# Elementwise binary cross entropy on one core: loads of predictions issued from SyncE instead of GpSimd

## The chip, the cores and the metric

The kernel runs on one core of one Trainium2 chip. The metric is the device time of one execution in microseconds (us); of several runs the median is given. The engines that matter here are VectorE (DVE), ScalarE (ACT), GpSimd (POOL) and SyncE (SP), and the 16 DMA engines of the core that carry all transfers between the memory (HBM) and the core's on-chip memory (SBUF, 128 partitions). An engine issues a transfer, and the transfer then stands in that engine's DMA queue.

## The reference

```
pred, target: float32 [8192, 8192]; pred in (0.01, 0.99), target 0 or 1
pred = clip(pred, 1e-7, 1 - 1e-7)
out  = -(target * log(pred) + (1 - target) * log(1 - pred))
```

With a target of 0 or 1 this is -log|target - 1 + pred|, and this form is what the kernel computes. Two inputs are read and one output is written, 268.4 MB each.

## The kernel before, in words

The 8192 x 8192 elements are taken as one flat list and cut into 39 chunks. A chunk of width w is 128 x w elements, row p of it on partition p, and contiguous in memory. Chunk 0 has w = 8192 (`first`), chunks 1 to 35 have w = 14336 (`WIDE`, called full chunks), and the last three, 36 to 38, have the widths of `TAIL`: 6656, 6656 and 1024. `z` is 35, the last full chunk.

Predictions live in `ring_p`, float32, with three slots of 14336 columns. Chunk k stands in slot k mod 3, and the three tail chunks lie side by side in one slot, that of chunk 33. All work on a chunk is done in place, and the store reads the same slot, so a slot is free again when the store of its chunk has landed. Targets live in `ring_t`, bfloat16 (the transfer converts from float32), with one single slot.

Per chunk, in two halves: `clip` (VectorE, L85), `merge` (VectorE, L91: target - 1 + pred), absolute value and logarithm (ScalarE, L94 and L95), `negate` (VectorE, L99). Then the chunk is stored (`store`, L79).

The order is written out by hand under a manual schedule: each engine carries out its instructions in the order of the text, and waits are put in where data or a slot demands them. In the loop over k the text reads: merge of chunk k, load of targets k+1 (`load_t`, L73, free to go when both merges have read the single slot), negate of k, clip of k+1, store of k, load of predictions k+2 (`load_p`, L70). Before the loop stand the loads p_0 (from ScalarE), t_0 and p_1 (from GpSimd). After it come the loads of the three tail chunks, predictions and targets in turn, the store of chunk 35, and the tail chunks' own work; their three stores (the last one in three pieces of 108, 12 and 8 rows) are issued from SyncE.

All other transfers are issued from GpSimd. Its order in the loop is thus t_k+1, s_k, p_k+2, t_k+2, s_k+1, p_k+3 and so on (t targets, s store, p predictions), one line in which each issue also waits for those ahead of it. The load p_k+2 needs the slot of chunk k-1, so it needs s_k-1 to have landed.

Of the kernel before, what the change touches and what calls it, by code (L numbers as in the profile page):

```python
# [1 line left out]

# [4 lines left out]

EPS = 1e-7

WIDE = 14336  # L10
SLOTS = 3
TAIL = (6656, 6656, 1024)
ROWS = (108, 12, 8)


@with_exitstack
def kernel(
    ctx: ExitStack,
    tc: tile.TileContext,
    pred: bass.AP,  # L20
    target: bass.AP,
    out: bass.AP,
):
    nc = tc.nc
    fp32 = mybir.dt.float32
    low = mybir.dt.bfloat16
    Alu = mybir.AluOpType
    Act = mybir.ActivationFunctionType
    P = nc.NUM_PARTITIONS

    R, C = pred.shape
    total = R * C // P
    rest = total - sum(TAIL)
    n = rest // WIDE
    first = rest - n * WIDE
    assert 0 < first <= WIDE and n > 4 and sum(TAIL) <= WIDE
    spots = [(first, 0)]
    spots += [(WIDE, k % SLOTS * WIDE) for k in range(1, n + 1)]
    c = (n + 1) % SLOTS * WIDE
    for w in TAIL:  # L40
        spots.append((w, c))
        c += w
    n = len(spots)
    z = n - 1 - len(TAIL)
    starts = [sum(w for w, _ in spots[:k]) * P for k in range(n)]

    pool = ctx.enter_context(tc.tile_pool(name="rings", bufs=1))
    ring_p = pool.tile([P, SLOTS * WIDE], fp32, name="ring_p", tag="ring_p")
    ring_t = pool.tile([P, WIDE], low, name="ring_t", tag="ring_t")
    warm = pool.tile([1, 8], fp32, name="warm", tag="warm")  # L50

    def chunk(ap, k):
        flat = ap.rearrange("r c -> (r c)")
        w = spots[k][0]
        return flat[starts[k] : starts[k] + w * P].rearrange("(p w) -> p w", p=P)

    def cols(ring, k, part, c):
        w = spots[k][0]
        i, m = part
        return ring[:, c + i * w // m : c + (i + 1) * w // m]  # L60

    def p_of(k, part=(0, 1)):
        return cols(ring_p, k, part, spots[k][1])

    def t_of(k, part=(0, 1)):
        return cols(ring_t, k, part, spots[k][1] % WIDE)

    def load_p(k):
        queue = nc.scalar if k == 0 else nc.gpsimd
        queue.dma_start(out=p_of(k), in_=chunk(pred, k))  # L70

    def load_t(k):
        nc.gpsimd.dma_start(out=t_of(k), in_=chunk(target, k))  # L73

    def store(k):
        queue = nc.sync if k > z else nc.gpsimd
        r = 0
        for rows in ROWS if k == n - 1 else (P,):
            queue.dma_start(out=chunk(out, k)[r : r + rows, :], in_=p_of(k)[r : r + rows, :])  # L79
            r += rows  # L80
        assert r == P

    def clip(k, *part):
        p = p_of(k, *part)
        nc.vector.tensor_scalar(  # L85
            out=p, in0=p, scalar1=EPS, scalar2=1 - EPS, op0=Alu.max, op1=Alu.min
        )

    def merge(k, *part):
        p, t = p_of(k, *part), t_of(k, *part)  # L90
        nc.vector.scalar_tensor_tensor(  # L91
            out=p, in0=t, scalar=1.0, in1=p, op0=Alu.subtract, op1=Alu.add
        )
        nc.scalar.activation(out=p, in_=p, func=Act.Abs)  # L94
        nc.scalar.activation(out=p, in_=p, func=Act.Ln)  # L95

    def negate(k, *part):
        p = p_of(k, *part)
        nc.vector.tensor_scalar(out=p, in0=p, scalar1=-1.0, scalar2=None, op0=Alu.mult)  # L99

    halves = (0, 2), (1, 2)
    with tc.manual_schedule():
        load_p(0)
        load_t(0)
        load_p(1)
        nc.vector.memset(warm, 1.0)  # L106
        nc.scalar.activation(out=warm, in_=warm, func=Act.Ln)  # L107
        for h in halves:
            clip(0, h)
        for k in range(z):  # L110
            for h in halves:
                merge(k, h)
            load_t(k + 1)
            for h in halves:
                negate(k, h)
            for h in halves:
                clip(k + 1, h)
            store(k)
            if k + 2 <= z:
                load_p(k + 2)  # L120
        for h in halves:
            merge(z, h)
        a, b, c = range(z + 1, n)
        for j in a, b, c:
            load_p(j)
            load_t(j)
        negate(z, halves[0])
        clip(a)
        negate(z, halves[1])
        store(z)  # L130
        merge(a)
        clip(b)
        merge(b)
        negate(a)
        store(a)
        clip(c)
        merge(c)
        negate(b)
        store(b)
        negate(c)  # L140
        store(c)


# [1 line left out]
_INS = ['pred', 'target']  # L145
_OUTS = [((8192, 8192), 'float32')]


# [23 lines left out]
```

## Time and profile before

| | before |
|---|---|
| median of 3 runs | 1867.39 us (1866.88 to 1868.22) |
| the profiled execution | 1868.84 us |
| its span (first to last instruction) | 1867.1 us |
| VectorE busy | 1118.2 us (60%) |
| ScalarE busy | 901.7 us (48%) |
| GpSimd busy | 283.3 us (15%) |
| moved by DMA | 671.14 MB, counted by what is written for the converted targets |
| issues of predictions at L70 from GpSimd | 38, median 3.82 us |
| issues of targets at L73 from GpSimd | 39, median 0.53 us |
| issues of stores at L79 from GpSimd / SyncE | 36, median 3.63 us / 5 |

How to read it: the profile is of one execution, whose own time is 1868.84 us; the span leaves out 1.7 us around the instructions. Issuing a transfer counts as busy time of GpSimd, the transfer itself does not. In a timeline a row gives the start and length in us, the engine, the line of the kernel, the operation with its tiles, and in brackets how long the engine had been idle before it and what ended that. "To landing" is the time from the issue of a transfer until its completion was signalled, so it includes the time that it stood in line. Besides these views, the trace holds a record of every DMA packet: its queue, its start, its length and its bytes. Here a packet is one row of a transfer.

### The profile page before, as it was taken

What the parts mean: (1) busy time and instruction counts of PE and PEld (TensorE: products, weight loads), DVE (VectorE), ACT (ScalarE), POOL (GpSimd) and SP (SyncE); (2) the same over time, 40 slices, a digit from 0 to 9 for tenths busy, and PEclk for the clock granted to TensorE, in tenths of its full rate; (3) what the DMA queues carried; (4) which work ended last, traced back from release to release, by engine and by line L of the source; (5) the groups of instructions that cost most, each with busy time, mean ns of one, the idle gap of its engine ahead of it and who ended that gap; (6) DMA issues with size and microseconds to landing.
All of it is one profiled execution on the core that took longest, in us unless ns stands there. A gap on an engine that the chain in (4) does not pass through costs nothing.

```text
span 1867.1 us, 695 instructions
## 1 busy us (share of the span) xinstructions
DVE 1118.2 (60%) x226; ACT 901.7 (48%) x152; POOL 283.3 (15%) x117
## 2 busy tenths in 40 slices
DVE  4675665655556555665665556655566665556664
ACT  3555444444555555444444555555544444455555
POOL 0121111111111101111111111101111111111100
DMA  9999999999999999999999999999999999999998
GB/s 331 336 373 373 364 355 359 356 355 355 354 354 359 373 373 373 370 356 362 356 354 358 354 354 356 367 373 373 373 362 360 359 354 359 354 354 354 360 366 346
DMA packets 16869, 671.14 MB, mean 359 GB/s; under 512 B 1888, under 2 KB 1888, under 8 KB 2272
## 3 DMA queue, kind: packets, MB, share of 16 engines
q0 software_dynamic: 16272, 659.56, 98.5%
q1 hardware_dynamic: 448, 7.34, 0.9%
q10 hardware_dynamic: 144, 4.19, 0.6%
q14 instruction: 5, 0.04, 0.0%
HBM read 536.87 MB, written 268.44 MB: 431 GB/s over the span
## 4 chain that ended last, share of the span: by engine, by line
DMA 67%; issue 28%; DVE 2%; ACT 2%; POOL 0%; POOLq 0%; DVEq 0%; PEldq 0%
DMA ring_t<-in_target_dram 67%; DVE ring_p L91 2%; ACT ring_p L95 1%; ACT ring_p L94 1%; DVE ring_p L99 0%; POOL out_dram L79 0%; POOL ring_p L70 0%; DVEq L167 0%; POOLq L73 0%; POOLq L79 0%; DVEq L91 0%; PEldq L167 0%
## 5 line engine op out<-in xcount | busy, mean ns | idle before, releaser
L94 ACT ACTIVATE ring_p<-ring_p 128x7168 f32<-128x7168 f32 (+3 forms) x75 | 451.6, 6021 | 943.5 <-DVE ring_p L91 943.5
L91 DVE SCALAR_TENSOR_TENSOR ring_p<-ring_t,ring_p 128x7168 f32<-128x7168 bf16 (+3 forms) x75 | 554.8, 7436 | 236.9 <-DMA ring_t<-in_target_dram 236.8
L99 DVE TENSOR_SCALAR ring_p<-ring_p 128x7168 f32<-128x7168 f32 (+3 forms) x75 | 285.0, 3801 | 475.0 <-ACT ring_p L95 475.0
L95 ACT ACTIVATE ring_p<-ring_p 128x7168 f32<-128x7168 f32 (+3 forms) x75 | 452.1, 6028 | 2.4
L85 DVE TENSOR_SCALAR ring_p<-ring_p 128x7168 f32<-128x7168 f32 (+3 forms) x75 | 281.8, 3798 | 20.1 <-DMA ring_p<-in_pred_dram 20.1
L79 POOL DMA_DIRECT2D out_dram<-ring_p x36 | 127.4, 3540 | 730.3 <-DVE ring_p L99 730.3
L73 POOL DMA_DIRECT2D ring_t<-in_target_dram x39 | 20.7, 532 | 802.9 <-DVE ring_p L91 802.1
L70 POOL DMA_DIRECT2D ring_p<-in_pred_dram x38 | 135.3, 3560 | 0.0
L107 ACT ACT_TABLE_LOAD x1 | 1.3, 1283 | 1.1 <-PEq L156 1.1
L106 DVE MEMSET warm<- 1x8 f32 x1 | 0.1, 65 | 0.8 <-PEq L156 0.8
L107 ACT ACTIVATE warm<-warm 1x8 f32<-1x8 f32 x1 | 0.2, 208 | 0.0
L156 POOL MEMSET const-float32-0.0<- 128x1 f32 x1 | 0.1, 98 | 0.2 <-issue 0.2
L156 POOL MEMSET const-bfloat16-1.0<- 128x1 bf16 x1 | 0.1, 101 | 0.0
L156 POOL MEMSET const-float32-1.0<- 128x1 f32 x1 | 0.1, 98 | 0.0
L156 POOL MEMSET const-uint8-127<- 128x1 uint8 x1 | 0.1, 98 | 0.0
## 6 DMA issues: line engine op xcount, KB each, us to landing
ring_p<-in_pred_dram POOLq DMA_DIRECT2D x35, 7168.0 KB, 44.3
out_dram<-ring_p POOLq DMA_DIRECT2D x35, 7168.0 KB, 31.0
ring_t<-in_target_dram POOLq DMA_DIRECT2D x35, 3584.0 KB, 35.2
ring_p<-in_pred_dram POOLq DMA_DIRECT2D x2, 3328.0 KB, 33.6
out_dram<-ring_p SPq DMA_DIRECT2D x2, 3328.0 KB, 15.1
ring_p<-in_pred_dram ACTq DMA_DIRECT2D x1, 4096.0 KB, 19.5
out_dram<-ring_p POOLq DMA_DIRECT2D x1, 4096.0 KB, 21.4
ring_t<-in_target_dram POOLq DMA_DIRECT2D x2, 1664.0 KB, 28.8
```

What stands on the lines that cost most here:

```text
L70: queue.dma_start(out=p_of(k), in_=chunk(pred, k))
L73: nc.gpsimd.dma_start(out=t_of(k), in_=chunk(target, k))
L79: queue.dma_start(out=chunk(out, k)[r : r + rows, :], in_=p_of(k)[r : r + rows, :])
L85: nc.vector.tensor_scalar(out=p, in0=p, scalar1=EPS, scalar2=1 - EPS, op0=Alu.max, op1=Alu.min)
L91: nc.vector.scalar_tensor_tensor(out=p, in0=t, scalar=1.0, in1=p, op0=Alu.subtract, op1=Alu.add)
L94: nc.scalar.activation(out=p, in_=p, func=Act.Abs)
L95: nc.scalar.activation(out=p, in_=p, func=Act.Ln)
L99: nc.vector.tensor_scalar(out=p, in0=p, scalar1=-1.0, scalar2=None, op0=Alu.mult)
L106: nc.vector.memset(warm, 1.0)
L107: nc.scalar.activation(out=warm, in_=warm, func=Act.Ln)
L156: nc = _bacc.Bacc("TRN2", target_bir_lowering=False, num_devices=1)
```

## The change

The predictions of chunks 2 to 35 are issued from SyncE; p_0 stays on ScalarE, p_1 and those of the three tail chunks stay on GpSimd. Targets and stores are issued as before.

```diff
     def load_p(k):
-        queue = nc.scalar if k == 0 else nc.gpsimd
+        queue = nc.scalar if k == 0 else nc.gpsimd if k == 1 or k > z else nc.sync
         queue.dma_start(out=p_of(k), in_=chunk(pred, k))
```

The orders of VectorE and ScalarE are the same in both kernels. GpSimd's list loses 34 issues and keeps the rest in order. SyncE's list begins with the 34 loads p_2 to p_35, and its stores of the tail chunks come after them. On SyncE the first of the loads, p_2, waits for nothing; each later one, p_k, waits for s_k-3, the store that frees its slot, and no longer stands behind s_k-2 as it did on GpSimd.

## The prediction

> **What bounds the kernel now.** I write p_k, t_k and s_k for the load of predictions, the load of targets and the store of chunk k. First I read the slices, the DMA queues and the HBM line of the page.
>
> ```profile
> span 1867.1 us, 695 instructions
> ...
> DMA  9999999999999999999999999999999999999998
> ...
> q0 software_dynamic: 16272, 659.56, 98.5%
> ...
> HBM read 536.87 MB, written 268.44 MB: 431 GB/s over the span
> ```
>
> The 16 DMA engines are busy in every slice, and nearly all of it is one queue, GpSimd's. VectorE (60%) and ScalarE (48%) have time to spare. Second, the timeline of a period in the steady part, from one target landing to the next:
>
> ```profile
> 306.61 15.16 DVE L91 SCALAR_TENSOR_TENSOR ring_p<-ring_t,ring_p 128x7168 f32<-128x7168 bf16 x2 [7.56 <-DMA ring_t<-in_target_dram]
> ...
> 322.06 0.53 POOL L73 DMA_DIRECT2D ring_t<-in_target_dram  x1 [22.90 <-DVE ring_p L91]
> ...
> 342.76 7.70 DVE L85 TENSOR_SCALAR ring_p<-ring_p 128x7168 f32<-128x7168 f32 x2
> 343.14 3.63 POOL L79 DMA_DIRECT2D out_dram<-ring_p  x1 [20.55 <-DVE ring_p L99]
> 346.76 3.82 POOL L70 DMA_DIRECT2D ring_p<-in_pred_dram  x1
> 357.39 15.16 DVE L91 SCALAR_TENSOR_TENSOR ring_p<-ring_t,ring_p 128x7168 f32<-128x7168 bf16 x2 [6.93 <-DMA ring_t<-in_target_dram]
> ```
>
> The reader is to see a period of 357.39 - 306.61 = 50.78 us, and three offsets from the target's landing that the change leaves alone: the next target is issued 15.45 us after it, the store 36.5 us after it, the old load of predictions 40.15 us after it. VectorE waits for the target (7 us a period), so the chain of waits is 67% "DMA ring_t". Is that target late by its own delay, or because the engines are full? The packet records decide: every DMA of 128 rows puts 8 rows on each engine; a row of 57,344 bytes takes 2.116 us, a target row (57,344 bytes read, 28,672 written) 2.130. One period is 8 x (2.116 + 2.116 + 2.130) = 50.90 us per engine, the period itself (packets overlap a little). So the steady part has no free DMA time, and nothing that is only issued earlier can shorten it. Third, the issues with time to landing:
>
> ```profile
> ring_p<-in_pred_dram POOLq DMA_DIRECT2D x35, 7168.0 KB, 44.3
> out_dram<-ring_p POOLq DMA_DIRECT2D x35, 7168.0 KB, 31.0
> ring_t<-in_target_dram POOLq DMA_DIRECT2D x35, 3584.0 KB, 35.2
> ...
> ring_p<-in_pred_dram ACTq DMA_DIRECT2D x1, 4096.0 KB, 19.5
> ...
> ring_t<-in_target_dram POOLq DMA_DIRECT2D x1, 2048.0 KB, 21.4
> ```
>
> A transfer needs 8 x 2.12 = 17 us alone; 31 to 44 us to landing means that it stands in line behind one or two others. In one line each transfer has 14 to 27 us of such cover. The last two rows are p_0 (ScalarE's queue) and t_0 (GpSimd's): 8 packets of 1.21 us each would be 9.7 us, and both took twice that, because two queues share each engine: in the packet records they alternate, one packet of each. That is the model for what follows. A packet is also chosen about one packet ahead: s_36, issued from SP at 1838.73, still saw some engines begin another packet of GpSimd's line at 1841.35, 2.6 us later, and come to it only after that.
>
> **The change, part by part.** *Removed*: 34 of the 38 issues at L70 leave GpSimd, 34 x 3.82 = 130 us of its time. Worth 0: GpSimd waits 802 us for VectorE at L73 and 730 at L79, and the engines have over 14 us of queued work whenever a store is issued. The store's 3.63 us against the target's 0.53 is time held back by the clip (342.76 to 350.46). [...]
>
> *Moved*: p_k+2 now waits on SP only for its slot, that is for s_k-1 to land. Behind it on SP stand only later predictions and the last stores. p_2 waits for nothing and starts at 0.7 us.
>
> *Start.* p_0, t_0 and p_2 now share the engines: 9.7 + 9.8 + 17 = 36.5 us from 1.8 on, so t_0 lands near 39 us (now 22.6). p_1 and t_1 follow in GpSimd's line, to 56 and 73. s_0 is issued 23.5 us after t_0's landing, at 62.5, in time, and runs from 73 to 82.7. Now both lines are empty: p_3 waits for s_0, and t_2 is issued only at 73.3 + 15.45 = 88.8. Gap 1 is landing to SP's issue (0.3 + 0.15), issue to first packet as for p_0 (0.73 to 1.74 and 2.49, so 1.0 to 1.8), and about 0.7 to 1.0 of a first packet (p_0's took 1.9 instead of 1.21): 2.5 us. p_3 and t_2 end near 119.5; s_1, issued at 110, fills 119.5 to 136.4; t_3 is issued at 119.8 + 15.45 = 135.3. How long a GpSimd issue takes to its first packet is bounded by two rows: t_0, issued at 1.23, has its first packet at 6.05 (4.8 us, in the cold start, and it had to wait its turn behind p_0); s_1, issued at 94.14, follows t_2's last packet without a gap at 100.1, 5.97 us after its issue, of which 3.62 were held back by the clip, so at most 2.4 us. I take 2, from the second, which is a warm queue. Gap 2: 135.3 + 2 - 136.4 = 0.9, with the first packet 1.5 us (0 to 4).
> [...]
>
> *Steady part.* p_4 becomes visible about 2 us after s_1 has ended, t_3 before that. So from then on the target leads by two packets (4.2 us), alternates with the predictions, and lands when these have two packets left; they fill the next store's stretch to 16.9 + 4.2 = 21.1 us after the target's last packet; the next target is visible 0.3 + 15.45 + 2 = 17.8 us after it, 3.3 us in time. This state feeds itself, and costs no gap. What it costs is the alternation: p_0's packets took 1.213 us alone and 1.226 between t_0's; 0.013 x 8 x 33 = 3.4 us. Bounds 0 and 3.4; I take 3.4.
>
> *End.* The last p from SP is p_35. With t_34 landing at 0, s_33 and the rest of p_35 run to 20.8, and t_35 alone to 37.9 (SP's line is empty). s_34 is issued only at 36.5, held back to 40.1 by the clip, first packet at about 42; p_36 stands behind it on GpSimd. Gap 3: 4 us (3, up to 6 if predictions have one packet left instead of two). Before, s_34 was issued 14 us before t_35's landing. From s_34's first packet to the end it is the same line in both kernels, full to the last stores, so the gap is not given back.
>
> **Sum** against the profiled execution (1868.84 us; span 1867.1): gaps 2.5 + 1.5 + 4 = 8.0; the gap of 1.0 us at 56 us (between t_1 and s_0) is counted half, since no row names its cause: -0.5; alternation 3.4; together +10.9: 1879.7. The median of the runs is 1.45 lower than that execution: 1878. By the lower ends (2.0 + 0 + 3 - 1 + 0 = 4) 1871, by the upper ends (3.3 + 4 + 6 + 3.4 = 16.7) 1884.
>
> **Rivals.** *Predictions lead.* If the target's first packet came over 3.5 us after its issue, p_k+2 would be there first in every period, end first, leave nothing for the store's stretch, and the engines would stand after each store until the freed slot is reloaded: 0.3 + 0.15 + 1.0 to 1.8, and about 1 us because the last packet of an emptied line ends later (t_1's at 56.7: 3.1 us instead of 2.13): 2.7 us x 32 periods = 86, and with 2.5 + 8 + 3.4 of the ends 100: 1967. For it speaks t_0's 4.8 us, against it s_1's 2.4. Chance 0.13. A mixture, some engines or some periods in this state, 1890 to 1940: 0.05.
> *Not slower.* Two packet sizes (32,768 bytes in 1.213 us, 57,344 in 2.116) give 0.009 us a packet that does not grow with the bytes. If two lines hid it, on the 16 alternating packets of 33 periods, 4.8 us would come back in place of 3.4 lost: +8.0 - 0.5 - 4.8 - 1.45 against 1868.84 is 1870, within 0.2% of now; it decides as soon as alternating packets are shorter than 2.116. Against it: p_0's and t_0's were longer. Chance 0.09. With the gaps at their lower ends as well it would be faster by 0.2%: 0.03; there is not more to gain, since the packet records show the engines short of their full rate for some 10 us of the span only, 3 of them at the start and 4 at the end.
>
> **How the numbers follow.** Forecast 0.70, predictions lead 0.13, mixture 0.05, not slower 0.09, faster 0.03. A measurement here tells 0.2% (3.7 us) from no change. Slower: 0.70 + 0.13 + 0.05 = 0.88; same 0.09; faster 0.03. The range from 1867 to 1900 holds the forecast with its bounds, the not-slower case and a little of the mixture; it leaves out the predictions' lead.
>
> **What would show it.** Right: VectorE's first clip at about 35 us; t_3's landing near 168 us (152.5 now); a period of 50.8 to 50.9; loads of predictions landing some 36 us after issue, targets 33 to 36; a gap near 83 us and one of some 4 us some 85 us before the end. Wrong: a period of 53 us with predictions landing before targets (first rival); packets of predictions under 2.116 us (second); a period under 50.7 would overturn the bound itself.

## The result, and the profile after

The changed kernel takes 1946.66 us (median of 4 runs, 1940.92 to 1950.99), the kernel before beside it 1867.81 us: a ratio of 1.0423, 95% interval 1.0406 to 1.044. It is slower, as forecast, but by 79 us instead of 10.6, and outside the range of 1867 to 1900. The profiled execution of the changed kernel took 1940.92 us, 72.1 more than the one of before.

The page's head, queues and HBM line:

```profile
span 1939.1 us, 731 instructions
...
DMA  9999999999999999999999999999999999999989
...
q0 software_dynamic: 11376, 410.00, 66.4%
q1 hardware_dynamic: 5344, 256.90, 32.1%
...
HBM read 536.87 MB, written 268.44 MB: 415 GB/s over the span
```

A third of the DMA time has moved to SyncE's queue (q1). The busy digits still say 9 in all slices but one; the loss shows only in the rate, 415 GB/s instead of 431. A packet that takes longer than usual counts as busy for its whole length, so most of this loss can't be seen in the busy share: over the 31 periods counted below it is 1.00 in both kernels, while the bytes written fall from 362 to 348 GB/s. The timeline of a period in the steady part:

```profile
1665.59 0.53 POOL L73 DMA_DIRECT2D ring_t<-in_target_dram  x1 [28.00 <-DVE ring_p L91]
1669.49 52.59 SPq L70 DMA_DIRECT2D ring_p<-in_pred_dram  x2
...
1686.67 3.63 POOL L79 DMA_DIRECT2D out_dram<-ring_p  x1 [20.55 <-DVE ring_p L99]
1702.77 15.16 DVE L91 SCALAR_TENSOR_TENSOR ring_p<-ring_t,ring_p 128x7168 f32<-128x7168 bf16 x2 [8.78 <-DMA ring_t<-in_target_dram]
...
1718.23 0.53 POOL L73 DMA_DIRECT2D ring_t<-in_target_dram  x1 [27.93 <-DVE ring_p L91]
```

From one target issue to the next it is 52.64 us here, and 50.8 before. The offsets of the issue and the store behind the merge's start are what they were. The longer part is the target's way from issue to landing, as the issues show:

```profile
out_dram<-ring_p POOLq DMA_DIRECT2D x35, 7168.0 KB, 35.4
ring_p<-in_pred_dram SPq DMA_DIRECT2D x34, 7168.0 KB, 38.7
ring_t<-in_target_dram POOLq DMA_DIRECT2D x35, 3584.0 KB, 37.3
```

The chain of waits has the same two links in both kernels (start, length). First the kernel before, then the changed one:

```profile
1592.17 35.18 DMA ring_t<-in_target_dram
...
1627.38 15.49 issue
```

```profile
1612.88 37.16 DMA ring_t<-in_target_dram
...
1650.08 15.50 issue
```

The reader is to see that the view can't tell the two apart. A loop "target on its way, merge, issue of the next target" closes in both. Before, the target has DMA work of others ahead of it, and the loop waits for the full engines. After, the engines wait for the loop, as the experiments with a shorter loop show.

Where the 72.1 us lie follows from the starts of the merges. Call the first merge of chunk k m_k:

| | before | after | difference |
|---|---|---|---|
| m_3 (start) | 152.6 | 171.7 | +19.1 |
| m_34 - m_3, 31 periods | 1576.3 (50.85 each) | 1637.7 (52.83 each) | +61.4 |
| m_34 to the end of the span | 138.1 | 129.8 | -8.3 |

### The profile page after: what moved, and what is told of

It reads as the page before. It is cut to its first block, busy times and chain, and to the rows that moved or that the text cites. A ratio compares the mean times of both kernels' runs of the same rounds, so it can differ in the third digit from the quotient of the medians.

```text
span 1939.1 us, 731 instructions
## 1 busy us (share of the span) xinstructions
DVE 1118.2 (58%) x226; ACT 901.6 (46%) x152; POOL 153.7 (8%) x83
## 4 chain that ended last, share of the span: by engine, by line
DMA 66%; issue 27%; ACT 4%; DVE 3%; POOLq 0%; DVEq 0%; PEldq 0%
DMA ring_t<-in_target_dram 66%; DVE ring_p L91 2%; ACT ring_p L95 2%; ACT ring_p L94 2%; DVE ring_p L99 0%; DVE ring_p L85 0%; DVEq L167 0%; POOLq L73 0%; POOLq L79 0%; DVEq L91 0%; PEldq L167 0%
## 5 line engine op out<-in xcount | busy, mean ns | idle before, releaser
L70 POOL DMA_DIRECT2D ring_p<-in_pred_dram x4 | 5.4, 1352 | 0.0
```

## The experiments

Theory A: a loop sets the period. The links are measured from the merge's start on, means over 28 periods of the changed kernel, with the slowest of the 16 engines taken at each link: 15.46 us to the next target's issue, 3.59 to its first packet, 30.85 from there to the end of its last packet, 2.50 until its last completion is written, 0.44 until the merge starts. The sum is 52.84, the period 52.82. That they agree shows nothing by itself: the links run from one merge to the next, so they add up to the period in every kernel, also in the one before. What differs is the link in which a target can wait for others. From its issue to its first packet on the fastest engine it is 13.9 us in the kernel before, where a line of other work stands ahead, and 1.4 in the changed one, where the line is nearly always empty. Theory B, the first rival: each completion, or each change of transfer, costs a fixed time where two queues share an engine, and the loop has nothing to do with it. In the packet records one engine's order in the changed kernel is this (T target, P predictions, S store, us each; one engine near 1667 us):

```
S2.12  T2.73 T2.13 P2.13 T2.13 P2.13 T2.13 P2.13 T2.13 P2.13 T2.13 P2.13 T2.13 P2.13 T2.13  P2.91 P2.12 S2.12 S2.12 ...
```

The target leads by two packets, as forecast, and packets are stretched in two places: the target's first (late: it is issued at 1665.59, and the first engine's line ends at 1666.49) and one of the predictions beside the target's completion. What the packets take beyond 2.13 us is 1.51 us a period in the mean of the engines, 0.69 with targets and 0.82 with predictions; before it is 0.03. For another 0.47 us a period the engines stand idle (before: 0.03). Together that is nearly the whole excess of the period, 52.83 - 50.85 = 1.98.

The kernels, with the period (the mean of the 31 from m_3 to m_34), m_3 and the stretch from m_34 to the end from the profiled execution (us):

| kernel | median (range, runs) | period | m_3 | m_34 to end |
|---|---|---|---|---|
| e1: after, merges on 1/2 | 1876.07 (1875.53 to 1877.07, 3) | 50.94 | 169.2 | 126.9 |
| e10: after, merges on 3/4 | 1879.12 (1876.91 to 1882.14, 3) | 50.94 | 170.5 | 127.6 |
| e9: after, merges on 7/8 | 1889.45 (1889.14 to 1889.75, 2) | 51.13 | 174.2 | 128.7 |
| after | 1946.66 (1940.92 to 1950.99, 4) | 52.83 | 171.7 | 129.8 |
| e11: after, loop longer | 1997.94 (1997.12 to 1998.76, 2) | 54.51 | 176.0 | 129.6 |
| e2: before, merges on 1/2 | 1869.06 (1867.64 to 1871.47, 8) | 50.91 | 152.0 | 138.8 |
| e12: before, loop longer | 1867.31 (1866.96 to 1868.95, 8) | 50.86 | 152.8 | 136.0 |
| e3: after, predictions in quarters | 1909.04 (1901.14 to 1916.95, 2) | 51.70 | 159.8 | 152.7 |
| e4: predictions from ScalarE, later | 1895.54 (1892.39 to 1899.61, 4) | 51.29 | 171.5 | 129.2 |
| e5: after, p_2 from GpSimd | 1939.89 (1934.38 to 1945.40, 2) | 53.08 | 168.4 | 129.8 |
| e6: before, p_2 from SyncE | 1885.01 (1884.93 to 1885.09, 2) | 50.85 | 168.8 | 138.1 |
| e7: after, predictions in halves | 1904.02 (1878.82 to 1909.34, 4) | 51.80 | 164.5 | 132.9 |
| e8: e7, p_2 and p_35 from GpSimd | 1877.91 (1871.81 to 1903.01, 7) | 50.69 | 162.4 | 139.5 |

**e1 and e2: a loop shorter by 7.5 us.** In the merge, on the changed kernel (e1) and on the one before (e2):

```diff
+        w = p.shape[-1] // 2 if k <= z else p.shape[-1]
         nc.vector.scalar_tensor_tensor(
-            out=p, in0=t, scalar=1.0, in1=p, op0=Alu.subtract, op1=Alu.add
+            out=p[:, :w], in0=t[:, :w], scalar=1.0, in1=p[:, :w], op0=Alu.subtract, op1=Alu.add
         )
```

> The changed kernel, but each merge (L91) of the full chunks works on the first half of its columns only, so half of the targets is left out of the result; ScalarE still works on all columns. VectorE's two merges then take some 7.7 us instead of 15.2, and the next target is issued 7.9 us after a landing instead of 15.45. Theory A (the loop from a target's landing over merge and issue to the next landing sets the period, and it became too long because a target's completion stands its turn behind a packet of predictions, 2 to 3 us): the loop has 7 us to spare, the period falls from 52.7 to 51 or 52 us and the time to 1880 to 1895. Theory B (each completion in a shared engine costs a fixed bubble, whenever the next transfer is issued): the period stays at 52 to 53 us, the time at 1930 or more.

> The kernel before with the same shortened merges, as the control (half of the targets of the full chunks is left out). Both theories: there the loop has 14 us to spare already, DMA sets the period of 50.8 us, so 1864 to 1869 us.

e1 gains nearly all of the loss, more than theory A had expected: ratio to the kernel before 1.0045 (1.0029 to 1.0061), period 50.94. The stretched packets are gone too (0.03 us a period), though completions are as many as in the changed kernel. Theory B falls with that. A shorter merge also brings the store's issue forward, by 3.7 us, but the store stands behind the target in GpSimd's line: it is issued 36.5 us after a merge's start in the changed kernel, and the target's last packet ends 49.9 us after it. The control does not move (1.0007, 0.9997 to 1.0017). What is left of e1 against before is the start and the end (+17 and -11) and some 0.1 us a period.

**e9, e10, e11 and e12: the dose.** e9 and e10 are e1 with `* 7 // 8` and `* 3 // 4` in place of `// 2`; e11 (on after) and e12 (on before) add an operation between the second merge and the next target:

```diff
                 merge(k, h)
+            t = t_of(k, halves[1])
+            nc.vector.tensor_scalar(out=t, in0=t, scalar1=1.0, scalar2=None, op0=Alu.mult)
             load_t(k + 1)
```

> The changed kernel with merges of the full chunks on 7/8 of their columns (an eighth of the targets is left out), so that the next target is issued 1.9 us earlier after a landing. Theory A says that the loop merge to issue (15.46 us) to first packet (3.59) to last packet (30.85) to completion (2.50) to merge (0.44) is the period of 52.8 us; taking 1.9 off gives 50.9, where DMA's own 50.85 takes over: period 50.9 to 51.3, time 1876 to 1892 us. Rival (a state of the engines, stretched packets, of which the early target is only one cure and needs several us): a period above 52, the time above 1915.

> As e9 with 3/4 of the columns (a quarter of the targets is left out): 3.8 us earlier. Theory A: no more to gain than at 7/8, DMA sets the period: 50.85 to 51, time 1874 to 1884 us. Rival: in between, 51.5 to 52.3, time 1895 to 1920.

> The changed kernel with one more VectorE operation on the target slot (multiplication by one, 128 x 7168 bfloat16) between the second merge and the issue of the next target, some 1.9 to 3.7 us by the rate of the clips. Theory A: the loop and the period grow by just its length, as nothing else sets the period: 54.7 to 56.5 us, time 2000 to 2065. Rival: the engines set the period, which stays within 0.5 us of 52.8: 1935 to 1960 us.

> The kernel before with the same operation, as the control. Its target has some 14 us of cover in the one queue, so the period stays at 50.8 and the time at 1865 to 1870 us under both theories.

The doses as measured are -1.87 and -3.74 us (merge to issue 13.59 and 11.72 instead of 15.46) and +2.06. The timeline of e11 shows the last one, the added row L114 ahead of the target's issue:

```profile
993.45 15.16 DVE L91 SCALAR_TENSOR_TENSOR ring_p<-ring_t,ring_p 128x7168 f32<-128x7168 bf16 x2 [10.68 <-DMA ring_t<-in_target_dram]
...
1008.64 2.03 DVE L114 TENSOR_SCALAR ring_t<-ring_t 128x7168 bf16<-128x7168 bf16 x1
1010.30 0.33 SPq L70 DMA_DIRECT2D ring_p<-in_pred_dram  x1
1010.96 0.53 POOL L73 DMA_DIRECT2D ring_t<-in_target_dram  x1 [31.88 <-DVE ring_t L114]
...
1047.75 15.16 DVE L91 SCALAR_TENSOR_TENSOR ring_p<-ring_t,ring_p 128x7168 f32<-128x7168 bf16 x2 [10.45 <-DMA ring_t<-in_target_dram]
```

The periods are 52.83, 51.13, 50.94 and 50.94 for 0, -1.87, -3.74 and -7.5: 1.70 us less for the first 1.87, then the floor of 50.9 that DMA sets. The times of e9 and e10 lie in theory A's ranges. So the loop sets the changed kernel's period, and its excess is just under 2 us, which is why an eighth of the merge suffices.

The other direction is no dose of the same loop, although its numbers, 54.51 us and 1997.94, came just below the range of theory A. The same added operation costs the kernel before nothing (ratio 0.9997, 0.9985 to 1.0008). In e11, though, SyncE now issues the predictions 0.66 us ahead of the target (1010.30 and 1010.96 above; in the changed kernel 3.90 behind it, 1669.49 and 1665.59), and the order of packets turns over. One engine of e11 from 992 us on:

```
S2.13 S2.12 S2.12 S2.12 S2.12 S2.12 S2.12 S2.12 (idle 2.41) P2.75 P2.12 T2.13 P2.13 T2.13 P2.13 T2.13 P2.13 T2.13 P2.13 T2.13 P2.13 T2.13 P2.13 T2.13 T2.64
```

In every steady period of e11 the predictions lead, by 4.7 to 5.0 us, and the target's packets come last. The engines stand idle for 2.11 us a period, mostly between the store and the reload of its slot. That is the prediction's rival "predictions lead", reached here by a later issue, at 3.7 us a period instead of the 2.7 at which it was priced. By the order of the packets, the next store, the gap and then 16 packets of predictions and target fill this period, and the merge is not among them. So the 1.68 us for 2.06 is no slope, and how near theory A's number came is luck. No run varies the added time within this order.

**e3, e7 and e8: shorter packets of predictions.** e3 with m = 4, e7 with m = 2:

```diff
-        queue.dma_start(out=p_of(k), in_=chunk(pred, k))
+        m = 4 if 2 <= k <= z else 1
+        for i in range(m):
+            w = spots[k][0] // m
+            queue.dma_start(out=p_of(k, (i, m)), in_=chunk(pred, k)[:, i * w : (i + 1) * w])
```

> The changed kernel, each load of predictions issued from SyncE in four transfers of a quarter of the columns, so that its packets have 14,336 bytes (about 0.54 us) instead of 57,344 (2.12 us). Theory A: a target's completion then waits for 0.5 us instead of 2 to 3, and its packets alternate with short ones, so it lands after some 22 us of transfer; the period falls to about 51 us, the time to 1875 to 1890, and the delay from a target's last packet to its landing to under 1.5 us. Theory B: there are four completions of predictions where there was one, so the bubbles grow: not under 1940 us, up to 2000.

In e3 the target's completion came 0.36 us after its last packet instead of 2.50, as theory A has it, but the time fell only halfway, to 1909, outside both expected ranges (ratio 1.0223, 1.0173 to 1.0273), with periods from 43.8 to 70 us. The waits of e3 (who waited for what: us in total, times, longest; its lines are three higher) name the new wait:

```profile
DVE ring_p L88 <- DMA ring_p<-in_pred_dram: 294.9, 17, 26.4
POOL ring_t L76 <- DMA ring_p<-in_pred_dram: 133.6, 3, 45.1
DVE ring_p L94 <- DMA ring_t<-in_target_dram: 14.3, 3, 11.6
```

The wait for targets has nearly gone (14.3 us), and the clip, L88, waits for predictions (294.9): with one packet each in turn, as in the engine's order above, the short packets would get a fifth of the time, 0.54 of 0.54 + 2.13 us; that share is an estimate from the lengths. Theory A's range left this out.

> The changed kernel, each load of predictions issued from SyncE in two transfers of half the columns (packets of 28,672 bytes, about 1.06 us). Theory A: the target's completion waits for one short packet (1.1 us instead of 2.1 to 2.9), its packets get two thirds of the time while it runs, so it ends some 4 us earlier against the predictions; the loop of 52.7 us becomes shorter than DMA's 50.9 and the period falls to 51 us, with the start and the end as in the changed kernel: 1873 to 1886 us, and no late predictions as with quarters. Rival (the two queues on one engine lose time by themselves, the stretched packets at each change of transfer): more transfers, more changes, no better than 1935 us.

> As e7 (halves), but p_2 and p_35 are issued from GpSimd, so that the start is not shared and the last full target has predictions in its own line. Theory A with gaps at the start and the end as terms of their own: 8 to 20 us less than e7, of which 3 to 4 at the end, that is 1862 to 1870 us, no better than the kernel before by more than 0.2%, since DMA is full. If the ends are not separate terms: the same as e7 within 3 us.

Halves give anything from 1879 to 1909 us in four runs (ratio 1.015, 1.008 to 1.022), e8 from 1872 to 1903 in seven (1.0065, 1.004 to 1.0091). Of these, one run of e7 lies in the range expected of it and none of e8. The completion came 1.1 us after the last packet in both, as expected. The profiled execution of e8 (1875.17 us) has a period of 50.8 in nearly every round and hardly a stretched packet (0.05 us a period), the one of e7 (1904.94 us) 51.8 with 0.81. The better runs agree with theory A, but the scatter is wider than any difference that these two were to show, so they settle nothing by themselves. No version with more predictions on a second queue beats the kernel before.

**e4: another queue, but later.** Predictions are issued from ScalarE behind the logarithms of chunk k:

```diff
-        queue = nc.scalar if k == 0 else nc.gpsimd if k == 1 or k > z else nc.sync
+        queue = nc.scalar if k == 0 else nc.gpsimd if k == 1 or k > z else nc.scalar
...
             load_t(k + 1)
+            if k + 2 <= z:
+                load_p(k + 2)
...
             store(k)
-            if k + 2 <= z:
-                load_p(k + 2)
```

> The loads of predictions from the third on are issued from ScalarE, behind the logarithms of chunk k, some 32 us after a target's landing instead of when their slot is free; the queue is another one than GpSimd's, as in the changed kernel. The predictions then share the engines with the store more than with the target. Theory A: the target is issued and carried early as in the kernel before, the start and the end have no new gaps, so 1866 to 1875 us, period 50.8 to 51. Theory B: store and predictions alternate, and their completions cost the bubbles all the same: 1900 to 1940 us.

1895.54 us lies between the two expectations. Periods go up and down between 46 and 58 us, 51.29 in the mean, and m_3 is at 171.5 as in the changed kernel: some 5 to 6 packets of predictions per engine run beside the target of one round and 3 to 4 beside that of the next, and the target's completion lags its last packet by 2.33 us. Issuing later did not keep the two apart, as I had thought it would.

**e5 and e6: the start alone.** e5 is the changed kernel with `k <= 2` in place of `k == 1`; e6 is the kernel before with p_2 alone on SyncE:

```diff
-        queue = nc.scalar if k == 0 else nc.gpsimd
+        queue = nc.scalar if k == 0 else nc.sync if k == 2 else nc.gpsimd
```

> The changed kernel with p_2 issued from GpSimd again, behind s_0 as in the kernel before; p_3 to p_35 stay on SyncE. It takes the crowding of the start away and nothing else. Theory A, with the start as a cost of its own: the third target lands some 15 us earlier than in the changed kernel (157 instead of 171.7 us), the period stays at 52.5 to 53, the time is 1922 to 1936. If the start decided which state the loop falls into (the rival of the prediction in which predictions lead), the period itself would change by 1 us or more, and the time with it by over 30 us.

> The kernel before with p_2 alone issued from SyncE at the start. Theory A: the start alone, with p_0, t_0 and p_2 sharing the engines, t_0 landing at 42 us and a gap behind s_0 until t_2; the third target lands near 166 us instead of 152.6, the period stays at 50.8: 1876 to 1884 us. If the start cost nothing because the DMA work done early is saved later: 1864 to 1870.

e6 is 18 us slower than before (ratio 1.0093, 1.0073 to 1.0114), just above the expected range, and nearly all of it lies ahead of m_3 (+16.2). Its timeline shows why:

```profile
38.35 4.50 DVE L85 TENSOR_SCALAR ring_p<-ring_p 128x4096 f32<-128x4096 f32 x2 [37.49 <-DMA ring_p<-in_pred_dram]
...
74.68 15.16 DVE L91 SCALAR_TENSOR_TENSOR ring_p<-ring_t,ring_p 128x7168 f32<-128x7168 bf16 x2 [3.11 <-DMA ring_t<-in_target_dram]
...
90.14 0.53 POOL L73 DMA_DIRECT2D ring_t<-in_target_dram  x1 [22.26 <-DVE ring_p L91]
...
111.22 3.63 POOL L79 DMA_DIRECT2D out_dram<-ring_p  x1 [20.55 <-DVE ring_p L99]
114.84 3.82 POOL L70 DMA_DIRECT2D ring_p<-in_pred_dram  x1
```

The first clip starts at 38.35 instead of 20.21, since p_0 and t_0 share the engines with p_2, and the DMA time won by that runs out after s_0: t_2 is issued at 90.14, s_1 only at 111.22. The shared start has a price of its own. But e5, without it, is not much better (1939.89, above the expected 1936; m_3 at 168.4 instead of the 157 that I expected): there p_3 on SyncE shares the engines with p_2, t_2 stands behind p_2 in GpSimd's line, and t_2's merge starts at 118.03, 60.7 us after t_1's. So the two queues cost the start 16 to 19 us whichever load is the first on SyncE (m_3 +16.2 in e6, +15.8 in e5, +19.1 in the changed kernel). The period of e5, 53.08, is within 0.3 us of the changed kernel's, so the start does not decide how the rest of the run goes.

## Why the prediction was wrong

*What bounds the kernel before*: right. The controls e2 and e12 take 7.5 us off its loop and add 2.06 to it, and it does not move. Nothing could be won, and nothing was.

*Removed issues*: right as far as the runs show. GpSimd is busy for 130 us less (283.3 to 153.7), and where the loop has slack (e1) the period is still no shorter than in the kernels before. No run shows the -0.5 that the sum has for the gap of 1.0 us at 56 us (-1 at its lower end). The gap was misread: from 55.7 to about 56.7 us all 16 engines were busy with the last packets of t_1, which took 2.8 to 3.3 us instead of 2.13.

*Start*: right in kind, short in size. The first clip was to start at about 35 us and started at 38.5; t_3 was to land near 168 us, and its merge started at 171.7. e5 shows that naming p_2's early start as the cause was too narrow.

*Steady part*: this is the step that failed: "the next target is visible 0.3 + 15.45 + 2 = 17.8 us after it, 3.3 us in time. This state feeds itself, and costs no gap." The order of packets was as said (the target leads by two, the predictions fill the store's stretch), but the loop in it was too short:

| link | predicted | measured |
|---|---|---|
| merge to issue of the next target | 15.45 | 15.46 |
| issue to first packet | 2 | 3.59 on the slowest engine (1.39 on the fastest) |
| first to last packet | 29.8 (8 + 6 packets) | 30.85 |
| last packet to merge | 0.3 | 2.50 + 0.44 |
| sum | 47.6 | 52.8 |

47.6 would have left DMA's 50.9 in charge, with the 3.3 us that the prediction claims. In its own terms: from the target's last packet to the next target's first one it has 17.8 us, against 21.1 until the line is empty. Measured are 2.50 + 0.44 + 15.46 = 18.4 and then 1.39 on the fastest to 3.59 on the slowest engine, so 19.8 to 22.0. The largest miss is the completion. I took 0.3 us from the kernel before, where the last completion came 0.00 us after a target's last packet. In the changed kernel's records a packet of predictions goes between the two. The last completion came 2.50 us after the last data packet in the changed kernel and 2.12 in e1, e9 and e10, about one packet of 2.13. It came 1.1 after it in e7 and e8, where packets of predictions take 1.06, and 0.36 in e3, where they take 0.54. In e11, where no packet of predictions is left by then, it came 0.00 after it. The second miss is that the 16 engines did not run in step: the landing came with the slowest one, and its first packet came 2.2 us after the fastest one's. The prediction also reads from one transfer, s_36 (packets of the other queue still begun 2.6 us after its issue), that a packet is chosen about one packet ahead, and does not use it: by this estimate, a target that is to follow without a stretched packet would have to be there one packet, 2.1 us, before the store's end. That is an argument; no run isolates it, nor how much of the excess each of the misses makes. The excess, 1.98 us x 31 = 61.4, is 85% of the loss.

*Alternation, 3.4 us*: in its bounds. Where the loop has slack (e1, e10) the period is 50.94 against 50.85 and 50.91 of the kernels before, 0.03 to 0.09 us x 31 = 1 to 3 us.

*End*: right. The gap between t_35's last packet (1846.7) and s_34's first (1850.1) is 3.4 us, against 4 predicted. The stretch from m_34 to the end is 8.3 us shorter, since s_34 comes sooner after m_34: its first packets begin 40.7 to 40.9 us after it (42 after the landing predicted), and 45.4 to 50.3 in the kernel before.

*Rivals*: predictions did not lead; the target's first packet came 1.2 us after its issue where the line was empty, so the question of 2.4 or 4.8 us, on which I put that rival's chance, was not the one that decided. But the changed kernel was close to it: in e11, with the target issued 2.06 us later, predictions lead throughout. The time of 1947 us lies between the forecast and that rival because the target's loop, and not the freed slot, ended last. No packet got shorter by alternating (2.13 in the middle of a transfer), so "not slower" falls.

Open: why packets are stretched by 0.8 us beside a target's completion in the changed kernel and not in e1. They go when the loop has slack, so they follow from its lateness here, but no run shows what holds them. Open too is why halves (e7, e8) scatter so widely.

## What to carry to other kernels

Before a transfer is moved to a second queue, follow the loop from a landing to the next landing of the same buffer, and put in it what was measured here with the second queue: packets of the two in turn (2.13 us each), a last completion 2.50 us after the last packet instead of 0.00, and a first packet on the slowest engine 2.2 us after the fastest one's. This loop had 14 us of cover in one queue and -2 in two. A busy DMA row and a chain of waits that names the same transfer did not tell here whether the engines wait for the loop or the loop for the engines: shorten the loop by 2 us, if only by leaving out work, and see whether the period follows. Lengthened, it can fall into another order of packets, as in e11, so the order has to be read before the numbers are compared. DMA time was full here (50.90 us of packets an engine in a period of 50.85): the earlier issue won nothing even where the loop had slack (50.94 in e1), and without that slack its order of packets made the period 52.83.

## What the runs showed of the hardware

In the kernel before, a target's last completion came 0.00 us after its last data packet. In the kernels with predictions on a second queue it came 2.1 to 2.5 us after it with packets of 57,344 bytes there (2.50 in the changed kernel, 2.12 in e1, e9 and e10), 1.1 with 28,672 (e7, e8), 0.36 with 14,336 (e3), and 0.00 where the other queue had none left (e11). In the changed kernel's records the packets of the two queues go one each in turn, 2.13 us each, while both have some. There a load issued from SyncE has its first packet 1.0 us after its issue on idle engines (p_3 at 84.0) and 3.4 to 4.8 us where the other queue has packets waiting; a target issued from GpSimd has it 1.2 us after its issue where its line is empty (1.39 in the mean of 28 periods). A store's issue from GpSimd took 3.63 us beside a clip, and 0.54 in e5 where it came ahead of the clip (93.91 and 96.67). In the changed kernel single packets of targets took up to 4.2 us and of predictions up to 3.8, instead of 2.13.
